# A bidirectional hybrid layer in fp32: one product form for the recurrent projections, one mask product a head, and another order at the start and in the middle norm

## The chip, the cores and the metric

The kernel runs on one core of one Trainium2 chip. The metric is the device time of one execution in microseconds (us). A core has TensorE (PE: matrix products and transpositions, with its weight loads, PEld), VectorE (DVE), ScalarE (ACT), GpSimd (POOL), and SyncE (SP), whose queue issues nearly all DMAs here.

## The reference

One layer on 256 tokens of width 2048, all in fp32:

```python
h = rmsnorm(x, g_pre)
xr, gr, q, k, v, qm, gl = split(h @ w_in)          # 2048 2048 2048 512 512 2048 3*2048
xc = conv4(xr) + b                                  # depthwise, along the tokens
y_lru  = (scan_forward(xc) + scan_backward(xc)) * gelu(gr)      # RG-LRU, gates from xc
y_attn = windowed_gqa(rope(q), rope(k), v)          # 16 heads of 128, |i-j| <= 128, sink logit
y_mem  = cross_attention(qm, rmsnorm(mem) @ w_mem_kv)           # 4 heads of 512
merged = sum(sigmoid(gl_b + b_gate) * (y_b @ w_b) for the three branches)
x = x + rmsnorm(merged @ w_out, g_post)             # "middle norm": this and the next
x = x + rmsnorm(square(relu(rmsnorm(x, g_mlp) @ w_up)) @ w_down, g_mlp_post)
```

## The kernel before, in words

Each fp32 operand of a product is split into a high part (rounded to TensorE's fp32r) and the remainder, and a product is three: high by high, high by low, low by high.

**Weights.** All weight matrices lie in one array of 344 chunks in the order of use, each of two halves of 128x1024 (512 KB). `emit` and `part` load a half on SP's queue (L113), ScalarE rounds it to `wh` (L117), VectorE subtracts to get `wl` (L119). There are six pairs of these tiles, three chunks. `chunk` takes the next one for use, `ahead` issues the one after next, and between the two calls of `emit` it runs `tick`: one step of each of the lists that `later` has put up. By these lists the vector work of the branches (convolution, gates, scans, softmax) is dealt out between the products, in program order on each engine.

**Two forms of a projection of 128 output features.** The activations `hm` of 128 input features are one tile of 512 columns, the high parts of the 256 tokens and then the low parts. `proj` (L157) takes a product of all 512 columns with `wh` for each of the 16 blocks of input features (L151), and one of the 256 high columns with `wl` (L155). Its bank then holds two halves that must be added: `ysum` copies one on ScalarE (L284) and adds the other on VectorE (L285). `proj_one` (L195) takes three products of 256 columns a block (L204 to L206) into half a bank; one VectorE multiplication with the reciprocal norm `rx` evacuates it. The start of the program makes four chunks block by block as the input lands (`quad`).

**Recurrent branch.** `lru_group` runs for four groups of four blocks of features. A group projects four chunks for `xr` and four for the gate `gl`. Group 0 has its `xr` from `quad`, so its form is `proj_one` for the four of `gl`; groups 1 to 3 use it for all eight. `hm` isn't normalized when these products are made, hence `rx` at the end.

**Windowed attention.** For a head and each of two token halves, `head_tasks` makes three products of 256 columns for the scores and adds the far block's mask by a product of a 128-column mask with the identity (L869 to L872).

**Order.** In most of the program a scheduler keeps the order of the code on each engine, with the lists above. In the start and in the middle norm the order of TensorE, ScalarE and VectorE is that of the code exactly.

**Start.** `first_act` loads the input (`xp`, four tiles of four blocks) and the first halves of weights in turn on SP (the first two blocks of `xp` and the two quarters of the first half apart), and TensorE meanwhile does products with ones (`warm`).

**Middle norm.** The last 512 columns of the output projection end in two banks `pst`, one for each half of the tokens (rows 0 and 1). A half's statistic gives `x1` by `x1_part` (L1075), `half_tiles` transposes it (L1086) and splits it, and `half_high` makes the first half products of four chunks of the MLP (L255) for one half of the tokens. The columns from 1024 on are transposed for both halves at once by `feed` (L1103). `quad_lows` and `quad_rest` (L263, L274) are the other products of the four chunks, and then come `proj` calls, the first into the bank that the oldest of the four chunks frees.

Of the kernel before, what the change touches and what calls it, by code (L numbers as in the profile page):

```python
# [15 lines left out]
P = 128  # L16
S = 256
# [46 lines left out]
class Body:  # L64
# [40 lines left out]
    def part(self, src, hi, lo, pieces=1, behind=None, keep=None, hook=None):  # L105
# [3 lines left out]
        for i in range(pieces):  # L109
            if hook is not None and 2 * i == pieces:  # L110
                hook()
# [14 lines left out]
    def emit(self, c, h, pieces=1, behind=None, keep=None, hook=None):  # L126
# [5 lines left out]
        return self.part(self.io["wall"][c, h], wh, wl, pieces, behind, keep, hook)  # L132
# [62 lines left out]
    def proj_one(self, act, spec, pool=None):  # L195
        nc = self.nc
        w = self.chunk(spec)
        ps = self.pmm.tile([P, 2 * S], F32, tag="mm", name="ps") if pool is None else pool.tile(
            [P, 2 * S], F32, tag="sc", name="ps")
        o = ps[:, :S]  # L200
        for k in range(KT):
            wh, wl = (x[:, (k % 8) * P:(k % 8 + 1) * P] for x in w[k // 8])
            a = act[k // 2][:, k % 2, :]
            nc.tensor.matmul(o, wh, a[:, :S], start=(k == 0), stop=False)  # L204
            nc.tensor.matmul(o, wh, a[:, S:], start=False, stop=False)  # L205
            nc.tensor.matmul(o, wl, a[:, :S], start=False, stop=(k == KT - 1))  # L206
        self.ahead()
        return o

    def tok_mms(self, pst, act, ci, w, ts, halves=(0, 1)):  # L210
        nc = self.nc
        for half in halves:
# [75 lines left out]

    def split(self, src, hi, lo):
# [36 lines left out]
    def setup_rest(self):  # L326
# [9 lines left out]
        self.masks = []  # L336
        for t in range(2):
# [7 lines left out]
            mr = c.tile([P, P], F32R, name=f"mask{t}")  # L345
            nc.vector.tensor_copy(mr, m)
            self.masks.append(mr)
# [158 lines left out]
    def first_act(self):  # L506
# [3 lines left out]
        self.warm(8)  # L510
# [10 lines left out]
        def half(i, hook=None):  # L521
            c, h = divmod(i, 2)
            firsts.append(self.emit(c, h, 1 if i else 2, firsts[i - 3] if i > 2 else None, hook=hook))
# [4 lines left out]
        def second():  # L528
            load(1, 1)
            tile_k(1)  # L530

        self.root_ready()
        load(0, 1)
        tile_k(0)
        half(0, second)
# [73 lines left out]
    def lru_group(self, g, hm, ylru, region=None):  # L609
# [26 lines left out]
        if g == 0:  # L636
# [5 lines left out]
            first = self.proj_one(hm, ("F", "w_in", D), self.psc)  # L642
# [4 lines left out]
        else:  # L647
            for b in range(4):
# [208 lines left out]
    def head_tasks(self, head, qa, ka, vh, vl, yattn):  # L857
# [4 lines left out]
        def scores():  # L862
            ps = self.psc.tile([P, 2, S], F32, tag="sc", name="sc")
            kh, kl = self.hl(ka, kv)
            for t in range(2):
                o = ps[:, t, :]
                far = ps[:, t, (1 - t) * P:(2 - t) * P]
                qh, ql = (x[:, t * P:(t + 1) * P] for x in qa)
                nc.tensor.matmul(o, qh, kh, start=True, stop=False)  # L869
# [446 lines left out]
```

## Time and profile before

| | us |
|---|---|
| median of 3 runs (lowest, highest) | 2013.94 (2012.83, 2014.39) |
| the profiled execution | 2013.35 |
| its span in the profile | 2011.6 |
| TensorE busy | 1996.1 (99%) |
| VectorE busy | 1264.4 (63%) |
| ScalarE busy | 1061.4 (53%) |

The span is from the first to the last instruction of the profile. Durations of products overlap, since TensorE is pipelined: its pace is read from starts. A wait is the idle time of an engine before an instruction, put down to what ended it.

### The profile page before, as it was taken

How to read it: one execution, taken by the hardware profiler on the slowest of the kernel's cores; microseconds unless marked ns; L12 is line 12 of the kernel's file. 1: busy time of each engine (PE TensorE's matmuls, PEld its weight loads, DVE VectorE, ACT ScalarE, POOL GpSimd, SP SyncE). 2: the span in 40 equal slices, each digit the busy share in tenths (PEclk: the TensorE clock that was granted, in tenths of full speed). 3: DMA queues.
4: the chain of work that ended last, by engine and by line, in shares of the span. 5: the costliest groups of instructions: out<-in, count | busy, mean ns of one | idle time of the engine just before them, and what ended most of it. 6: DMA issues, size and time to landing. Idle time of an engine off the chain costs nothing.

```text
span 2011.6 us, 27672 instructions
## 1 busy us (share of the span) xinstructions
PE 1996.1 (99%) x10700; PEld 1728.7 (86%) x10700; DVE 1264.4 (63%) x1629; ACT 1061.4 (53%) x1502; POOL 28.1 (1%) x30
## 2 busy tenths in 40 slices
PE   9999999999999999999999999999999999999998
PEld 8999998888888888888888888888888888888886
DVE  7988596876567555655655555575456556555654
ACT  6767667778344444544454444464445445434542
POOL 0000000000022000000000000000000000000000
PEclk9999999999999999999999999999999999999999
DMA  8665565554666655555556566366555555555563
GB/s 276 205 210 177 187 218 178 170 170 154 205 204 220 198 189 183 173 169 180 179 174 199 188 220 210 136 220 198 190 190 189 195 189 188 196 191 189 189 219 105
DMA packets 110405, 383.24 MB, mean 191 GB/s; under 512 B 12864, under 2 KB 15936, under 8 KB 110272
## 3 DMA queue, kind: packets, MB, share of 16 engines
q1 hardware_dynamic: 110128, 381.45, 57.9%
q8 instruction: 84, 1.38, 0.3%
q14 instruction: 49, 0.40, 0.1%
q10 hardware_dynamic: 144, 0.01, 0.0%
HBM read 376.69 MB, written 2.10 MB: 188 GB/s over the span
## 4 chain that ended last, share of the span: by engine, by line
PE 97%; DVE 1%; ACT 0%; DMA 0%; issue 0%; SPq 0%; DVEq 0%; ACTq 0%
PE ps L151 20%; PE pst L220 18%; PE pst L221 18%; PE pst L224 18%; PE ps L155 11%; PE ps L204 3%; PE ps L206 3%; PE ps L205 3%; DVE wl L119 1%; PE tp L830 0%; PE ps L255 0%; DMA xp<-xT 0%; PE gps L673 0%; PE av L843 0%; PE gps L672 0%
## 5 line engine op out<-in xcount | busy, mean ns | idle before, releaser
L119 DVE TENSOR_TENSOR wl<-raw,wh 128x1024 fp32r<-128x1024 f32 (+1 forms) x689 | 846.7, 1232 | 472.8 <-ACT wh L117 466.9
L117 ACT ACTIVATE wh<-raw 128x1024 fp32r<-128x1024 f32 (+1 forms) x689 | 726.2, 1057 | 582.4 <-PE pst L221 504.3
L151 PE MATMUL ps<-h,wh 128*128 128x512 f32 x960 | 229.8, 391 | 0.8 <-DVE y L285 0.8
L151 PEld LDWEIGHTS ps<-h,wh 128*128 128x128 f32 x960 | 176.3, 188 | 35.3 <-DVE y L285 1.2
L220 PE MATMUL pst<-wh,u 128*128 128x512 f32 x512 | 199.2, 389 | 0.0
L221 PE MATMUL pst<-wh,u 128*128 128x512 f32 x512 | 199.2, 389 | 0.0
L284 ACT ACTIVATE evac<-ps 128x256 f32<-128x256 f32 x120 | 45.3, 380 | 247.9 <-PE ps L151 247.9
L220 PE MATMUL pst<-wh,hm 128*128 128x512 f32 x416 | 163.1, 392 | 0.0
L221 PE MATMUL pst<-wh,hm 128*128 128x512 f32 x416 | 162.4, 390 | 0.0
L151 PE MATMUL ps<-hm,wh 128*128 128x512 f32 x576 | 142.8, 392 | 0.0
L224 PE MATMUL pst<-wl,u 128*128 128x512 f32 x512 | 137.5, 389 | 0.0
L204 PE MATMUL ps<-hm,wh 128*128 128x256 f32 x448 | 126.9, 283 | 0.4 <-DVE xr L285 0.4
L155 PEld LDWEIGHTS ps<-h,wl 128*128 128x128 f32 x960 | 123.1, 191 | 4.7
L205 PE MATMUL ps<-hm,wh 128*128 128x256 f32 x448 | 126.8, 283 | 0.0
L206 PE MATMUL ps<-hm,wl 128*128 128x256 f32 x448 | 126.8, 283 | 0.0
L155 PE MATMUL ps<-h,wl 128*128 128x256 f32 x960 | 124.5, 283 | 0.0
L151 PEld LDWEIGHTS ps<-hm,wh 128*128 128x128 f32 x576 | 104.1, 189 | 19.1
L221 PEld LDWEIGHTS pst<-wh,u 128*128 128x128 f32 x512 | 96.1, 188 | 20.0
L224 PEld LDWEIGHTS pst<-wl,u 128*128 128x128 f32 x512 | 96.1, 188 | 20.0
L220 PEld LDWEIGHTS pst<-wh,u 128*128 128x128 f32 x512 | 96.1, 188 | 19.9
L224 PE MATMUL pst<-wl,hm 128*128 128x512 f32 x416 | 111.2, 389 | 0.0
L285 DVE TENSOR_TENSOR y<-ps,evac 128x256 f32<-128x256 f32 x64 | 27.1, 424 | 106.6 <-ACT evac L284 106.6
(261 smaller groups left out, 3108.5 us busy)
## 6 DMA issues: line engine op xcount, KB each, us to landing
raw<-wall SPq DMA_DIRECT2D x687, 512.0 KB, 3.5
raw<-wgate SPq DMA_DIRECT2D x8, 512.0 KB, 4.1
bias<-bgate SPq DMA_DIRECT2D x12, 256.0 KB, 2.9
swap<-ry SPq DMA_DIRECT2D x40, 64.0 KB, 2.5
mp<-memT SPq DMA_DIRECT2D x4, 512.0 KB, 4.9
x<-xt SPq DMA_DIRECT2D x4, 512.0 KB, 4.7
out<-x SPq DMA_DIRECT2D x8, 256.0 KB, 2.1
xp<-xT SPq DMA_DIRECT2D x3, 512.0 KB, 7.2
```

The source lines that it names most:

```text
L117: act = nc.scalar.activation(hi[:, s], raw[:, s], AF.Copy)
L119: nc.vector.tensor_tensor(lo[:, s], raw[:, s], hi[:, s].bitcast(F32), op=ALU.subtract)
L151: self.nc.tensor.matmul(ps, wh, act[k // 2][:, k % 2, :], start=(k == 0), stop=(k == KT - 1))
L155: self.nc.tensor.matmul(ps[:, S:], wl, act[k // 2][:, k % 2, :S], start=False, stop=False)
L204: nc.tensor.matmul(o, wh, a[:, :S], start=(k == 0), stop=False)
L205: nc.tensor.matmul(o, wh, a[:, S:], start=False, stop=False)
L206: nc.tensor.matmul(o, wl, a[:, :S], start=False, stop=(k == KT - 1))
L220: nc.tensor.matmul(pst[t], xh, wh[i], start=(k == 0), stop=False)
L221: nc.tensor.matmul(pst[t], xl, wh[i], start=False, stop=False)
L224: nc.tensor.matmul(pst[t], xs[k, t][0], wl[i], start=False, stop=(k == KT - 1))
L284: self.nc.scalar.activation(t, ps[:, S:2 * S], AF.Copy)
L285: self.nc.vector.tensor_tensor(out, ps[:, :S], t, op=ALU.add)
```

## The change

There are five parts.

1. `proj_one` is gone. The 28 chunks that used it go through `proj`, with `ysum` behind it, and the multiplication by `rx` comes once for four chunks, on a whole page of 128x1024 (`by_rx`). `xr` of groups 1 to 3 is a page now, and its convolutions follow as steps of a list after all four chunks.
2. `proj` can take a bank of the other pool, `psc`. The first two gate chunks of group 0 and the fifth chunk of the MLP use it.
3. In the scores the two mask products of a head become one of 256 columns, over both token halves, between the products of the high and of the low parts of q.
4. In the middle norm the transpositions of the second block of row 0 move between the high and the low products of the last half of the output projection (`between`), those of row 1 move among the products of row 0, and the residuals of the later columns are made whole and earlier.
5. At the start the first half of the weights is one load, ahead of the input, the first two blocks of the input are one load, and `warm(8)` becomes `warm(10)`.

```diff
-    def proj(self, act, spec):
+    def proj(self, act, spec, pool=None):
         w = self.chunk(spec)
-        ps = self.pmm.tile([P, 2 * S], F32, tag="mm", name="ps")
+        ps = self.pmm.tile([P, 2 * S], F32, tag="mm", name="ps") if pool is None else pool.tile(
+            [P, 2 * S], F32, tag="sc", name="ps")
...
+            if between is not None:
+                between()
...
+    def by_rx(self, page):
+        r = self.rx.unsqueeze(1).broadcast_to([P, 4, S])
+        self.nc.vector.tensor_tensor(page, page, r, op=ALU.mult)
...
         self.root_ready()
-        load(0, 1)
+        lows = []
+        half(0, lows)
+        load(0, 2)
         tile_k(0)
-        half(0, second)
+        lows[0]()
+        tile_k(1)
         load(2, 2)
...
-                ps = self.proj_one(hm, ("F", "w_in", (4 * g + b) * P))
-                x = self.t1("xr")
-                nc.vector.tensor_tensor(x, ps, self.rx, op=ALU.mult)
-                self.later([lambda b=b, x=x: conv(b, x)])
+                self.ysum(self.proj(hm, ("F", "w_in", (4 * g + b) * P)), page[:, b, :])
+            self.by_rx(page)
+            self.later(*([lambda b=b: conv(b, page[:, b, :])] for b in range(4)))
...
-            ps = first if g == 0 and b == 0 else self.proj_one(hm, ("F", "w_in", D + (4 * g + b) * P))
-            nc.vector.tensor_tensor(gl[:, b, :], ps, self.rx, op=ALU.mult)
+            spec = ("F", "w_in", D + (4 * g + b) * P)
+            ps = first if g == 0 and b == 0 else self.proj(hm, spec, self.psc if g == 0 and b == 1 else None)
+            self.ysum(ps, gl[:, b, :])
+            if b == 3:
+                self.by_rx(gl)
...
-                nc.tensor.matmul(o, qh, kh, start=True, stop=False)
-                nc.tensor.matmul(far, self.identr, self.masks[t], start=False, stop=False)
-                nc.tensor.matmul(o, qh, kl, start=False, stop=False)
-                nc.tensor.matmul(o, ql, kh, start=False, stop=True)
+                nc.tensor.matmul(ps[:, t, :], q[t][0], kh, start=(t == 0), stop=False, skip_group_check=True)
+                nc.tensor.matmul(ps[:, t, :], q[t][0], kl, start=False, stop=False, skip_group_check=True)
+            far = ps.rearrange("p t s -> p (t s)")[:, P:P + S]
+            nc.tensor.matmul(far, self.identr, self.masks, start=False, stop=False, skip_group_check=True)
+            for t in range(2):
+                nc.tensor.matmul(ps[:, t, :], q[t][1], kh, start=False, stop=True, skip_group_check=True)
...
-            half_tiles(0, 1)
-            self.tok_mms(pst, mg, 3, pair[1], (1,), (1,))
+            self.tok_mms(pst, mg, 3, pair[1], (1,), (1,), lambda: half_tiles(0, 1))
             statistic(1)
...
-            self.half_high(ups, wup, h2, 0, range(8))
+            self.half_high(ups, wup, h2, 0, range(6))
...
             z_gain(1)
+            half_tiles(1, 0)
             z_gain(0)
-            half_tiles(1, 0)
+            self.half_high(ups, wup, h2, 0, range(6, 8))
+            self.half_high(ups, wup, h2, 1, range(1))
             half_tiles(1, 1)
-            self.half_high(ups, wup, h2, 1, range(8))
-            x1_part(1, rows[1], 2, near)
+            self.half_high(ups, wup, h2, 1, range(1, 8))
+            x1_part(1, rows[1], 2, full)
             low(1)
+            x1_part(0, rows[0], 3, full)
             feed(4)
...
-            x1_part(1, rows[1], 2, far)
             feed(5)
+            x1_part(1, rows[1], 3, full)
             low(1)
...
-                    ps = self.proj(h2, ("F", "w_up", q * D + n * P))
+                    ps = self.proj(h2, ("F", "w_up", q * D + n * P), self.psc if q == 0 and n == 4 else None)
```

Three places of the order on the engines. The first is VectorE within the chunks of the second group of the recurrent branch, before: `xr` and `xc` are the projection and its convolution, `T`, `ip` and `a` are pages of the scan's gates.

```order
L119 TENSOR_TENSOR wl<-raw,wh 128x1024
L623 SCALAR_TENSOR_TENSOR xc<-xr,vec,xc 128x254
L651 TENSOR_TENSOR xr<-ps,rstd 128x256
L291 TENSOR_TENSOR xca<-xc,xca 128x256
L119 TENSOR_TENSOR wl<-raw,wh 128x1024
L623 SCALAR_TENSOR_TENSOR xc<-xr,vec,xc 128x255
L119 TENSOR_TENSOR wl<-raw,wh 128x1024
L623 SCALAR_TENSOR_TENSOR xc<-xr,vec,xc 128x255
L623 SCALAR_TENSOR_TENSOR xc<-xr,vec,xc 128x254
L651 TENSOR_TENSOR xr<-ps,rstd 128x256
L712 TENSOR_TENSOR ip<-ip,T 128x1024
L291 TENSOR_TENSOR xca<-xc,xca 128x256
```

The same place after:

```order
L271 TENSOR_TENSOR xr<-ps,evac 128x256
L117 TENSOR_TENSOR wl<-raw,wh 128x1024 x2
L702 TENSOR_TENSOR ip<-ip,T 128x1024
L271 TENSOR_TENSOR xr<-ps,evac 128x256
L117 TENSOR_TENSOR wl<-raw,wh 128x1024
L277 TENSOR_TENSOR xr<-xr,rstd 128x1024
L117 TENSOR_TENSOR wl<-raw,wh 128x1024
L610 SCALAR_TENSOR_TENSOR xc<-xr,vec,xc 128x255 x4
L610 SCALAR_TENSOR_TENSOR xc<-xr,vec,xc 128x254 x2
L117 TENSOR_TENSOR wl<-raw,wh 128x1024
L281 TENSOR_TENSOR xca<-xc,xca 128x256
L271 TENSOR_TENSOR gl<-ps,evac 128x256
```

Each `xr` was multiplied out of its bank and convolved at once; now it is added (L271), the page is multiplied in one (L277), and the convolutions come together behind it.

The second is TensorE in the middle norm, from the last but one half of the output projection on, before. `mg` is the merged input of that projection, `ft` the transposed tiles, `x_11344` and `x_11173` the tiles of the norm's output, `h_...` the pairs of its transposed blocks.

```order
L224 MATMUL pst<-wl,mg 128x512 x2
L1086 MATMUL ft<-ident,x_11344 128x128 x4
L220 MATMUL pst<-wh,mg 128x512
L221 MATMUL pst<-wh,mg 128x512
L220 MATMUL pst<-wh,mg 128x512
L221 MATMUL pst<-wh,mg 128x512
L224 MATMUL pst<-wl,mg 128x512 x2
L255 MATMUL ps<-h_11789,wh 128x2x128 x8
L255 MATMUL ps<-h_11790,wh 128x2x128 x8
L255 MATMUL ps<-h_11791,wh 128x2x128 x8
L255 MATMUL ps<-h_11792,wh 128x2x128 x8
L1086 MATMUL ft<-ident,x_11173 128x128 x4
```

The same after, where the tiles are `x_10931` and `x_10760`:

```order
L210 MATMUL pst<-wl,mg 128x512 x2
L204 MATMUL pst<-wh,mg 128x512
L205 MATMUL pst<-wh,mg 128x512
L204 MATMUL pst<-wh,mg 128x512
L205 MATMUL pst<-wh,mg 128x512
L1076 MATMUL ft<-ident,x_10931 128x128 x4
L210 MATMUL pst<-wl,mg 128x512 x2
L241 MATMUL ps<-h_11376,wh 128x2x128 x8
L241 MATMUL ps<-h_11377,wh 128x2x128 x8
L241 MATMUL ps<-h_11378,wh 128x2x128 x8
L1076 MATMUL ft<-ident,x_10760 128x128 x4
L241 MATMUL ps<-h_11379,wh 128x2x128 x8
```

The first transpositions shown moved down behind four high products, and the two sets that followed the 32 half products (the second of them not shown before) now stand after 24 and after 36 of them.

The third is ScalarE's start, before: `hm` the split input, `wh` the rounded weights.

```order
L278 ACT_TABLE_LOAD
L278 ACTIVATE junk<-eps 128x1
L494 ACTIVATE hm<-xp,vec 128x256
L117 ACTIVATE wh<-raw 128x512
L494 ACTIVATE hm<-xp,vec 128x256
L117 ACTIVATE wh<-raw 128x512
L494 ACTIVATE hm<-xp,vec 128x256 x2
L117 ACTIVATE wh<-raw 128x1024
```

And after:

```order
L264 ACT_TABLE_LOAD
L264 ACTIVATE junk<-eps 128x1
L115 ACTIVATE wh<-raw 128x1024
L482 ACTIVATE hm<-xp,vec 128x256 x4
L115 ACTIVATE wh<-raw 128x1024
L482 ACTIVATE hm<-xp,vec 128x256 x2
```

The first half of the weights is rounded in one piece, before any of the input.

## Rows read from the trace of the kernel before

**Rows 1.** The page: busy time, share of the span and instructions of each engine.
```profile
PE 1996.1 (99%) x10700; PEld 1728.7 (86%) x10700; DVE 1264.4 (63%) x1629; ACT 1061.4 (53%) x1502; POOL 28.1 (1%) x30
```

**Rows 2.** Waits: engine, line, waited for; us in total, times, longest.
```profile
DVE y L285 <- ACT evac L284: 106.6, 58, 1.9
...
PE ft L1103 <- DVE x L1075: 2.2, 2, 1.4
PE ps L183 <- ACT wh L117: 2.2, 3, 1.4
...
PE ps L204 <- DVE xr L285: 0.4, 1, 0.4
DVE ry L285 <- ACT evac L284: 0.4, 1, 0.4
```

**Rows 3.** A window: start:end, us, busy us (instructions) of PE, PEld, DVE, ACT, POOL.
```profile
168.58:214.66 46.08, 46.08 (x386) 46.07 (x385) 44.31 (x65) 29.48 (x36) 0.00 (x0) 1.00 0.69 213
```

**Rows 4.** The chain in order of time: start us, us, what.
```profile
1478.52 3.65 PE ps L151 x16
...
1484.09 3.65 PE ps L151 x16
```

**Rows 5.** Instructions on tile xr: ns min/median/max, first and last start, forms.
```profile
L651 DVE TENSOR_TENSOR xr<-ps,rstd x12: 411/417/425, 91.2 to 276.6; 128x256 f32<-128x256 f32 x12
L285 DVE TENSOR_TENSOR xr<-ps,evac x4: 417/418/420, 38.1 to 39.1; 128x256 f32<-128x256 f32 x4
```

**Rows 6.** Timeline, VectorE and TensorE: start us, us, engine, line, operation.
```profile
113.32 1.22 DVE L119 TENSOR_TENSOR wl<-raw,wh 128x1024 fp32r<-128x1024 f32 x1
...
121.42 0.28 PE L206 MATMUL ps<-hm,wl 128*128 128x256 f32 x1
```

**Rows 7.** Timeline of TensorE at one head of the windowed attention.
```profile
449.27 0.60 PE L830 MATMUL tp<-ident,pr 128*128 128x128 f32 x4
449.62 0.36 PE L869 MATMUL sc<-kact,qa 128*128 128x256 f32 x1
...
450.64 0.40 PE L220 MATMUL pst<-wh,hm 128*128 128x512 f32 x1
```

**Rows 8.** Timeline of TensorE in the middle norm, and one row of VectorE.
```profile
1288.44 0.63 PE L224 MATMUL pst<-wl,mg 128*128 128x512 f32 x2
...
1289.76 0.48 PE L220 MATMUL pst<-wh,mg 128*128 128x512 f32 x1
...
1291.24 3.99 PE L255 MATMUL ps<-h,wh 128*128 128x256 f32 x32
...
1292.93 1.42 DVE L1075 SCALAR_TENSOR_TENSOR x<-z,tot,x 128x512 f32<-128x512 f32 x2
...
1295.06 1.09 PE L1086 MATMUL ft<-ident,x 128*128 128x128 f32 x8
1296.39 4.09 PE L255 MATMUL ps<-h,wh 128*128 128x256 f32 x32 [0.25 <-DVE h L495]
...
1318.78 1.09 PE L274 MATMUL ps<-h,wh 128*128 128x512 f32 x4
1320.66 1.66 PE L151 MATMUL ps<-h,wh 128*128 128x512 f32 x6 [0.78 <-DVE y L285]
```

**Rows 9.** Timeline of TensorE at the start.
```profile
0.99 3.79 PE L481 MATMUL warm<-ones 128*128 128x128 f32 x16 [0.99 <-POOL eps L309]
5.06 1.41 PE L183 MATMUL ps<-hm,wh 128*128 128x512 f32 x4 [0.28 <-ACT wh L117]
...
7.44 1.20 PE L183 MATMUL ps<-hm,wh 128*128 128x512 f32 x4 [0.49 <-ACT wh L117]
...
13.86 1.19 PE L183 MATMUL ps<-hm,wh 128*128 128x512 f32 x4
```

**Rows 10.** The chain at the start.
```profile
1.65 0.42 SPq L514
...
4.01 7.91 DMA xp<-xT
```

More of the change, by code (lines that the diff above doesn't have):

```diff
@@ L103, in drain, with part @@
             self.tick()
-    def part(self, src, hi, lo, pieces=1, behind=None, keep=None, hook=None):
+    def part(self, src, hi, lo, pieces=1, behind=None, keep=None):
         nc = self.nc
@@ L109, in part @@
         for i in range(pieces):
-            if hook is not None and 2 * i == pieces:
-                hook()
             s = slice(i * n, (i + 1) * n)
@@ L124, in part, with emit @@
         return act
-    def emit(self, c, h, pieces=1, behind=None, keep=None, hook=None):
+    def emit(self, c, h, pieces=1, behind=None, keep=None):
         if c >= NCH or (c, h) in self.held:
@@ L131, in emit @@
         self.held[c, h] = (wh, wl)
-        return self.part(self.io["wall"][c, h], wh, wl, pieces, behind, keep, hook)
+        return self.part(self.io["wall"][c, h], wh, wl, pieces, behind, keep)
     def ahead(self):
@@ L193, in quad, with tok_mms @@
         return ps
[L195 to L210, printed above, removed]
+    def tok_mms(self, pst, act, ci, w, ts, halves=(0, 1), between=None):
         nc = self.nc
@@ L335, in setup_rest @@
         nc.vector.tensor_copy(self.identr, self.ident)
-        self.masks = []
+        self.masks = c.tile([P, S], F32R, name="masks")
         for t in range(2):
@@ L344, in setup_rest @@
             )
-            mr = c.tile([P, P], F32R, name=f"mask{t}")
-            nc.vector.tensor_copy(mr, m)
-            self.masks.append(mr)
+            nc.vector.tensor_copy(self.masks[:, t * P:(t + 1) * P], m)
     def rates(self):
@@ L509, in first_act @@
         pages = [self.page_fp("xp") for _ in range(4)]
-        self.warm(8)
+        self.warm(10)
         nc.scalar.dma_start(self.vec[:, :KT], self.io["vec"][:, :KT])
@@ L519, in tile_k, with half @@
             self.scaled_split(pages[k // 4][:, k % 4, :], self.v("norm_mix_pre", k), *self.hl(hm, k))
-        def half(i, hook=None):
+        def half(i, keep=None):
             c, h = divmod(i, 2)
-            firsts.append(self.emit(c, h, 1 if i else 2, firsts[i - 3] if i > 2 else None, hook=hook))
+            firsts.append(self.emit(c, h, 1, firsts[i - 3] if i > 2 else None, keep=keep))
         def square(p):
             nc.scalar.activation(pages[p], pages[p], AF.Square)
-        def second():
-            load(1, 1)
-            tile_k(1)
         self.root_ready()
-        load(0, 1)
+        lows = []
+        half(0, lows)
+        load(0, 2)
         tile_k(0)
-        half(0, second)
+        lows[0]()
+        tile_k(1)
         load(2, 2)
@@ L641, in lru_group @@
                 self.ysum(pss[b], xs[b])
-            first = self.proj_one(hm, ("F", "w_in", D), self.psc)
+            first = self.proj(hm, ("F", "w_in", D), self.psc)
             self.token_scale()
@@ L647, in lru_group @@
         else:
+            page = self.page_fp("xr")
             for b in range(4):
-                ps = self.proj_one(hm, ("F", "w_in", (4 * g + b) * P))
-                x = self.t1("xr")
-                nc.vector.tensor_tensor(x, ps, self.rx, op=ALU.mult)
-                self.later([lambda b=b, x=x: conv(b, x)])
+                self.ysum(self.proj(hm, ("F", "w_in", (4 * g + b) * P)), page[:, b, :])
+            self.by_rx(page)
+            self.later(*([lambda b=b: conv(b, page[:, b, :])] for b in range(4)))
         for b in range(4):
-            ps = first if g == 0 and b == 0 else self.proj_one(hm, ("F", "w_in", D + (4 * g + b) * P))
-            nc.vector.tensor_tensor(gl[:, b, :], ps, self.rx, op=ALU.mult)
+            spec = ("F", "w_in", D + (4 * g + b) * P)
[3 more added lines that the diff above has]
+                self.by_rx(gl)
             if b % 2 == 0:
@@ L864, in scores @@
             kh, kl = self.hl(ka, kv)
+            q = [[x[:, t * P:(t + 1) * P] for x in qa] for t in range(2)]
             for t in range(2):
-                o = ps[:, t, :]
-                far = ps[:, t, (1 - t) * P:(2 - t) * P]
-                qh, ql = (x[:, t * P:(t + 1) * P] for x in qa)
-                nc.tensor.matmul(o, qh, kh, start=True, stop=False)
-                nc.tensor.matmul(far, self.identr, self.masks[t], start=False, stop=False)
-                nc.tensor.matmul(o, qh, kl, start=False, stop=False)
-                nc.tensor.matmul(o, ql, kh, start=False, stop=True)
+                nc.tensor.matmul(ps[:, t, :], q[t][0], kh, start=(t == 0), stop=False, skip_group_check=True)
[4 more added lines that the diff above has]
+                nc.tensor.matmul(ps[:, t, :], q[t][1], kh, start=False, stop=True, skip_group_check=True)
             box["ps"] = ps
@@ L1163, in run @@
             self.quad_lows(ups, wup, h2, range(4))
-            x1_part(1, rows[1], 2, far)
             feed(5)
+            x1_part(1, rows[1], 3, full)
             low(1)
             self.quad_lows(ups, wup, h2, range(4, 8))
-            x1_part(0, rows[0], 3, full)
             wup.append(self.chunk(ups_specs[2]))
             low(1)
-            x1_part(1, rows[1], 3, full)
             self.quad_rest(ups, h2, wup, range(8, 9))
```

## The prediction

> **What bounds the kernel now.** I read the busy shares first: TensorE 99% of the span, VectorE 63%, ScalarE 53% [rows 1]. So the change can pay only where TensorE works for less time or stands less; what happens on the other engines counts only if TensorE comes to wait for it. The waits come next [rows 2]: those of TensorE are short and lie at the start (2.2 us for weights in three waits, 0.4 us for `xr`) and in the middle norm (2.2 us for `x`). The largest of VectorE, 106.6 us in 58 waits for the copy of a product, holds up nobody, but it matters for a rival. Then I read the pace of the products in a window and in the chain, and last the gaps of TensorE in the middle norm and at the start.
>
> **Part 1, the 512-column form (28 chunks).** Before, eight such chunks are the window from 168.58 to 214.66, in which TensorE is never idle [rows 3]: 46.08 / 8 = 5.760 us a chunk, and 5.760 / 48 = 0.120 us a product of 256 columns. The other form, 16 products of 512 columns and 16 of 256, takes from 1478.52 to 1484.09 in the chain, where nothing waits: 5.567 us (3.65 / 16 = 0.228 and 1.91 / 16 = 0.119 a product) [rows 4]. TensorE saves 0.193 us a chunk, 28 x 0.193 = 5.4 us, all on the path that sets the end.
> The Trainium skill ("TensorE: Matmul & The Clock Gate", section "Back-to-back issue gap") gives N/2.4 + 2.5 ns as the gap of single products, with the remark that a stream can differ. An estimate from that page is 215.8 ns for 512 columns and 109.2 for 256, a saving of 0.04 us a chunk and 1.2 us in all. The rows have 228 and 120 ns, some 13 ns over the columns for each product and not 2.5, so the trace decides for the larger saving.
> The price is on VectorE. Each chunk had one multiply (417 ns) and now has one add (417 ns) [rows 5] that must wait for ScalarE's copy, and a group of four is then multiplied by the norm as one page of 128x1024. For this the nearest row is the subtraction of `wl`, of the same shape, at 1.22 us [rows 6]; I take that (it lies between 1.2 and four multiplies of 0.42, 1.7). A stretch of eight has two of them. VectorE is busy 44.31 of 46.08 us there [rows 3], so it wants 44.31 + 2.44 = 46.75 us in 46.08 - 1.55 = 44.53: 2.2 us too much. What hides it is the lead of the weights: a `wl` made from 113.32 to 114.54 is first used at 121.42, 6.9 us later [rows 6]. I take 0; without this cover it costs 3 x 2.2 = 6.6 us. It can't gain: VectorE does no less than before. ScalarE's eight copies more don't bind, it is busy 29.48 of 46.08 [rows 3].
> The second gate chunk of the first group gets a bank of the other pool, so TensorE need not wait for the bank that `xr` frees: 0.4 us [rows 2], and with it the restart, which at the end of the middle norm is 0.2 (0.97 us lost there for 0.78 waited, part 3). I take 0.6, between 0.3 and 0.8.
>
> **Part 2, the scores (16 heads).** A head's eight products take 449.62 to 450.64, 1.02 us [rows 7]. Six products of 256 columns and one mask product of 256, at 0.12 each, make 0.84; the first one behind transpositions may start 0.08 late as it does now. So 0.10 to 0.18 a head; I take 0.106, 16 x 0.106 = 1.7 us, between 0.8 (half of it lost at the changes of weights) and 2.9. Nothing else moves: the maximum over the scores reads the same bank as before.
>
> **Part 3, the middle norm.** Four transpositions among products take 0.35 us, as 449.27 to 449.62 shows for the same size [rows 7]. TensorE loses time in five places [rows 8]. 1288.44 to 1289.76 holds two low products (0.46) and four transpositions (0.35): 0.51 lost. 1295.06 to 1296.39 holds eight transpositions (0.70): 0.63 lost. The two waits for `x` at later transpositions are 2.2 us [rows 2] and, with a restart of 0.2 each, 2.6. 1318.78 to 1320.66 holds four products (0.91): 0.97 lost. In all 4.7 us, the most that can go.
> I follow the new order. The transpositions of half 0,1 stand behind the high products of the last half, when their `x` is there: the first place closes, and TensorE is done with the output projection at 1290.63 in place of 1291.24 [rows 8]. But the splits of these four blocks come some 0.2 us later, ScalarE takes the second statistic behind them, and the first residual of row 1, which now starts at 1292.93 and takes 0.71, is ready at about 1293.9. TensorE has done six of eight parts of the first half at 1290.63 + 6/8 x 3.82 = 1293.5 (3.82 = 1295.06 - 1291.24): 0.4 us of wait, and I add 0.25 (the wait at 1296.39) at the one part of the second half and again at the next transpositions, since both need splits just made. These 0.9 us eat what the first two places gave (1.1); the second half ends 0.1 to 0.2 earlier. Behind it the residuals of columns 1024 to 2047 are whole and come earlier, so the two waits for `x` go (2.6), and the fifth projection has a bank of its own, so the last wait goes (0.97). What is late next: the subtraction for the ninth chunk now stands behind a residual; I take 0.4 us of wait. Sum 0.15 + 2.6 + 0.97 - 0.4 = 3.3; I take 3.2. Bounds: -0.8 if the early waits are twice as long and the later ones stay, 4.7 if no new wait comes.
>
> **Part 4, the start.** The first half chunk is now one load ahead of `xp`, and the first two blocks of `xp` come as one. Before, TensorE starts products at 5.06 and 7.44 [rows 9], stands 2.2 us in three waits [rows 2], and begins its fifth group at 13.86. What must have landed for the first product now is what had to for the second group, so it moves from 5.06 to about 7.4 to 7.7, and the groups run on without the idle 2.2 us. The work of the first four groups is 13.86 - 5.06 - 2.2 = 6.6; from 7.7 it ends at 14.3, which is 0.5 later than before. The other end is all idle gone, 2.2 earlier. Two issues fewer stand ahead of the block that the chain waits for, at 0.42 us each; but the chain waits 7.91 us for its bytes [rows 10], which are as many as before, so I take half of that gain, 0.4 us (-0.5 to 2.2). The four more warm products end at about 5.7, before any data of the new order is there, and cost nothing.
>
> **Sum.** 5.4 + 0.6 + 1.7 + 3.2 + 0.4 = 11.3 us. The profiled execution took 2013.35 (span 2011.6 and 1.75 around it), so 2002.0. The median of the runs lies 0.6 above it, which I leave to the range.
>
> **The rivals.**
> All better: no new wait in the middle norm (4.7) and 2 us at the start: 2002.0 - 1.5 - 1.6 = 1998.9. For it: each wait that I added rests on a single row. Chance 0.08.
> The middle norm saves nothing, because the statistic of row 1 and not TensorE sets the time there: 2005.2. For it: VectorE and ScalarE have as much to do between the same two ends. Against it: the two longest waits [rows 2] are for late residuals that the new order moves ahead of subtractions not yet wanted. Chance 0.11.
> The start goes wrong: the products begin at the lower level of the clock (1.2 GHz), as TensorE now stands some 2 us between the warm products and the first group. Against it: an idle stretch of up to 1.4 us [rows 2] passed there, and the groups on both sides of it, at 7.44 and 13.86, took the same 1.2 us [rows 9]. The Trainium skill ("TensorE: Matmul & The Clock Gate", section "Why this matters for your kernels") says that idle gaps between bursts bring the lower clock back; no run here shows it. Half of the 6.6 us of work at half the clock costs 3.3 us and the 0.4 goes: 2005.7; with the change of level somewhat earlier, 2004.5. Chance 0.05.
> The 512-column form saves nothing, because columns alone set the pace and both forms have 12,288 of them in a chunk: 2002.0 + 5.4 = 2007.4. By the formula of the Trainium skill that part 1 quotes it would be 2006.2. Against it stand the two rates measured [rows 3, 4]. Chance 0.03.
> Slower: VectorE, which works in order, now waits for ScalarE's copy in each of the eight chunks. Where such adds wait, the mean is 106.6 / 58 = 1.84 us [rows 2]; eight make 14.7, with the overflow 16.9, less the lead of 6.9 it is 10 us a stretch, 30 in three: 2032. It decides once waits and overflow pass the 6.9 us of lead. For it: VectorE has 1.8 us to spare in 46. Against it: the 20 adds of `ry`, which stand among the same kind of work, waited 0.4 us in all [rows 2], since a busy VectorE comes to an add after the copy is done. Chance 0.06, half of it within 0.2% of before, where a third of that price is paid.
>
> **How the numbers follow.** Forecast 0.67, with a range of its own of 2000.0 to 2004.5. To hold the better case (0.08), the middle norm (0.11) and the start (0.05) as well, the range is 1999.0 to 2006.5; some 0.15 lies outside it. 0.2% (4 us) is about what a measurement can tell from no change. Faster by more than that: 0.67 + 0.08 + 0.11 + 0.05 + 0.03 = 0.94; within it 0.03; slower 0.03.
>
> **What would show it.** Eight chunks of the recurrent projections take 44.5 us with no wait of TensorE for `wl` or `xr`; a head's scores take 0.84 to 0.92; the wait for `x` at the later transpositions is gone, shorter waits (0.25 to 0.5) stand around the first two half products of the MLP, and from the end of the output projection to the fifth projection of the MLP it is some 2.6 us less; the first product comes at 7.3 to 7.7 and the fifth group at 13.4 to 13.9. A wait for `wl` or a copy in the stretches of eight would make the prediction wrong.

## The result and the profile after

The changed kernel takes 2002.26 us (median of 6 runs, 2001.10 to 2002.71), the kernel before 2013.65 (6 runs, 2012.83 to 2014.39): a ratio of 0.9943, 95% interval 0.993 to 0.9955, or 11.4 us less. The profiled execution after took 2002.71 us, with a span of 2000.9 (2011.6 before).

The page and the waits of the kernel after answer to [rows 1, 2]. The engines' busy shares hardly move, TensorE is busy for 7.3 us less:

```profile
PE 1988.8 (99%) x10240; PEld 1705.7 (85%) x10240; DVE 1270.2 (63%) x1634; ACT 1068.7 (53%) x1529; POOL 28.1 (1%) x30
```

Waits (engine, line, waited for: us in total, times, longest us):

```profile
DVE y L271 <- ACT evac L270: 107.0, 58, 1.9
...
PE ps L182 <- DVE hm L483: 1.6, 1, 1.6
...
PE ps L260 <- DVE wl L117: 0.2, 1, 0.2
```

The waits for `x` and for `xr` are gone from TensorE, the three at the start have become one of 1.6 us, and one of 0.2 us for a `wl` is new.

Where the time went is read best from the starts of the same work of TensorE in the two timelines:

| work of TensorE | before | after | earlier by | gained since the line above |
|---|---|---|---|---|
| first projection behind the four chunks of the start | 31.40 | 31.19 | 0.21 | 0.21 |
| sums for `rx`, behind that projection | 37.14 | 36.77 | 0.37 | 0.16 |
| second gate chunk | 38.56 | 37.44 | 1.12 | 0.75 |
| end of the last stretch of eight chunks | 299.49 | 293.28 | 6.21 | 5.09 |
| first scores | 354.95 | 348.71 | 6.24 | 0.03 |
| behind the windowed attention | 493.83 | 486.10 | 7.73 | 1.49 |
| first transposition of the middle norm | 1287.08 | 1279.35 | 7.73 | 0.00 |
| first down projection of the MLP | 1387.59 | 1376.27 | 11.32 | 3.59 |
| last down projection | 1915.91 | 1904.59 | 11.32 | 0.00 |

So TensorE gains 11.3 us in five places and nothing in between. From the last down projection to the end of the span it is 95.7 us before and 96.3 after, so the two profiled executions differ by a little less, 10.7. The change doesn't touch this last part: it takes 95.6 to 96.35 us in the fourteen traces of this document, without regard to the edit.

A stretch of eight chunks, to be held against [rows 3] (start:end, us, busy us of PE, PEld, DVE, ACT, POOL with instructions, then the granted clock):

```profile
165.48:210.01 44.53, 44.53 (x257) 39.37 (x256) 42.55 (x64) 30.92 (x43) 0.00 (x0) 1.00 0.66 206
```

It takes 44.53 us for 46.08, with 256 weight loads in the window in place of 385. VectorE is busy 42.55, not more than before.

A head, to be held against [rows 7]: the scores take 442.26 to 443.17, 0.91 us for 1.02.

```profile
441.91 0.60 PE L820 MATMUL tp<-ident,pr 128*128 128x128 f32 x4
442.26 0.36 PE L857 MATMUL sc<-kact,qa 128*128 128x256 f32 x1
...
443.17 0.40 PE L204 MATMUL pst<-wh,hm 128*128 128x512 f32 x1
```

The middle norm on TensorE, to be held against [rows 8]:

```profile
1282.99 3.04 PE L241 MATMUL ps<-h,wh 128*128 128x256 f32 x24
1286.16 0.65 PE L1076 MATMUL ft<-ident,x 128*128 128x128 f32 x4
1286.57 1.87 PE L241 MATMUL ps<-h,wh 128*128 128x256 f32 x12
1288.29 0.76 PE L1076 MATMUL ft<-ident,x 128*128 128x128 f32 x4
1288.80 3.59 PE L241 MATMUL ps<-h,wh 128*128 128x256 f32 x28
1292.23 0.60 PE L1093 MATMUL ft<-ident,x 128*128 128x128 f32 x4
...
1296.93 1.09 PE L260 MATMUL ps<-h,wh 128*128 128x512 f32 x4
1298.24 0.74 PE L260 MATMUL ps<-h,wl 128*128 128x256 f32 x4 [0.21 <-DVE wl L117]
...
1308.54 1.09 PE L260 MATMUL ps<-h,wh 128*128 128x512 f32 x4
1309.46 1.98 PE L149 MATMUL ps<-h,wh 128*128 128x512 f32 x8
```

The start, to be held against [rows 9], and the windows of it (the granted clock is the third figure from the end):

```profile
0.99 4.25 PE L469 MATMUL warm<-ones 128*128 128x128 f32 x20 [0.99 <-POOL eps L299]
6.88 1.20 PE L182 MATMUL ps<-hm,wh 128*128 128x512 f32 x4 [1.64 <-DVE hm L483]
8.02 1.17 PE L187 MATMUL ps<-hm,wl 128*128 128x256 f32 x4
8.98 1.91 PE L182 MATMUL ps<-hm,wh 128*128 128x512 f32 x4
...
14.35 1.09 PE L182 MATMUL ps<-hm,wh 128*128 128x512 f32 x4
```

```profile
7.00:8.00 1.00, 1.00 (x4) 0.55 (x4) 1.00 (x2) 0.65 (x2) 0.00 (x0) 1.00 1.04 414
8.00:9.00 1.00, 1.00 (x6) 0.98 (x6) 1.00 (x3) 0.65 (x2) 0.00 (x0) 0.55 1.01 414
9.00:11.00 2.00, 2.00 (x7) 1.61 (x7) 1.51 (x3) 0.67 (x1) 0.00 (x0) 0.50 1.04 412
11.00:12.00 1.00, 1.00 (x6) 0.92 (x6) 0.29 (x1) 0.83 (x3) 0.00 (x0) 0.74 1.00 401
12.00:14.00 2.00, 2.00 (x13) 1.73 (x12) 1.54 (x3) 2.00 (x5) 0.00 (x0) 1.00 0.92 348
```

The first group runs at the full clock. (The trace's first record of the granted clock stands at 4.69 us; ahead of a first record the column shows 1.00 whatever the pace. The warm products start 213 ns apart up to there and 111 behind it.) From some point past 8 us to past 11 us the granted clock is 0.50, the lower of the two levels, and four products of 512 columns take 1.7 us (8.98 to 10.69) in place of 0.93.

### The profile page after: what moved, and what is told of

Read it like the earlier page. It is cut to its first block, busy times and chain, and to the rows that moved or that the text cites. A ratio compares the mean times of both kernels' runs of the same rounds, so it can differ in the third digit from the quotient of the medians.

```text
span 2000.9 us, 26757 instructions
## 1 busy us (share of the span) xinstructions
PE 1988.8 (99%) x10240; PEld 1705.7 (85%) x10240; DVE 1270.2 (63%) x1634; ACT 1068.7 (53%) x1529; POOL 28.1 (1%) x30
## 4 chain that ended last, share of the span: by engine, by line
PE 99%; DVE 0%; DMA 0%; ACT 0%; issue 0%; DVEq 0%; SPq 0%; ACTq 0%
PE ps L149 26%; PE pst L205 18%; PE pst L204 18%; PE pst L210 18%; PE ps L153 13%; PE ps L182 1%; PE ps L260 1%; PE tp L820 0%; PE ps L187 0%; PE gps L663 0%; PE av L833 0%; PE gps L662 0%; PE av L832 0%; PE gps L661 0%; PE av L831 0%; PE ps L241 0%
## 5 line engine op out<-in xcount | busy, mean ns | idle before, releaser
L117 DVE TENSOR_TENSOR wl<-raw,wh 128x1024 fp32r<-128x1024 f32 x688 | 846.3, 1234 | 453.9 <-ACT wh L115 447.7
L115 ACT ACTIVATE wh<-raw 128x1024 fp32r<-128x1024 f32 x688 | 725.2, 1058 | 556.2 <-PE pst L205 500.4
L149 PE MATMUL ps<-hm,wh 128*128 128x512 f32 x1024 | 250.9, 392 | 0.0
L149 PEld LDWEIGHTS ps<-hm,wh 128*128 128x128 f32 x1024 | 186.4, 189 | 35.0
L270 ACT ACTIVATE evac<-ps 128x256 f32<-128x256 f32 x148 | 55.9, 380 | 268.6 <-PE ps L149 268.6
L153 PEld LDWEIGHTS ps<-hm,wl 128*128 128x128 f32 x1024 | 131.3, 191 | 5.1
L153 PE MATMUL ps<-hm,wl 128*128 128x256 f32 x1024 | 132.8, 283 | 0.0
L271 DVE TENSOR_TENSOR y<-ps,evac 128x256 f32<-128x256 f32 x64 | 27.2, 424 | 107.1 <-ACT evac L270 107.0
L210 PEld LDWEIGHTS pst<-wl,hm 128*128 128x128 f32 x416 | 78.1, 188 | 16.3
```

Of the source, the lines that this page charges most:

```text
L115: act = nc.scalar.activation(hi[:, s], raw[:, s], AF.Copy)
L117: nc.vector.tensor_tensor(lo[:, s], raw[:, s], hi[:, s].bitcast(F32), op=ALU.subtract)
L149: self.nc.tensor.matmul(ps, wh, act[k // 2][:, k % 2, :], start=(k == 0), stop=(k == KT - 1))
L153: self.nc.tensor.matmul(ps[:, S:], wl, act[k // 2][:, k % 2, :S], start=False, stop=False)
L210: nc.tensor.matmul(pst[t], xs[k, t][0], wl[i], start=False, stop=(k == KT - 1))
L270: self.nc.scalar.activation(t, ps[:, S:2 * S], AF.Copy)
```

## The experiments

Each is the changed kernel with one edit, unless it says more. Starts are compared with those of the changed kernel behind the start, since the start itself varies from one execution to the next, as the first four show.

**Warm products until the input is there.**

```diff
-        self.warm(10)
+        self.warm(18)
```

> The changed kernel with 18 pairs of warm products in place of 10, so that TensorE works until about 6.8 us and goes over to the first product at 6.88 without standing. In the changed kernel it stands 1.64 us there, and the granted clock is 0.50 to 0.55 from about 8.3 to 11.3 us. Theory (the idle time brings the lower clock; the landing of the last quarter of the input takes back a part): clock 1.00 throughout, the fifth group begins at 13.0 to 13.4 in place of 14.35, but the thirteenth must wait for its weights split at 24.9, so the first chunk behind the four begins 0.3 to 0.7 us earlier than 31.19; time 2001.6 to 2001.9. Rival 1 (nothing behind binds): 1.0 to 1.6 us earlier. Rival 2 (the clock falls whatever TensorE did before): clock 0.5 again, 0 us.

2001.98 us (5 runs, 2001.46 to 2002.42), ratio to before 0.9941 (0.9927 to 0.9954). TensorE begins the groups 0.8 us later and is through 1.0 us earlier:

```profile
7.65 1.17 PE L182 MATMUL ps<-hm,wh 128*128 128x512 f32 x4
8.66 0.63 PE L187 MATMUL ps<-hm,wl 128*128 128x256 f32 x4
...
30.17 1.98 PE L149 MATMUL ps<-hm,wh 128*128 128x512 f32 x8
```

The granted clock is 1.00 in every window, and its first record, at 6.52 us, is ahead of the first group. The first chunk behind the four comes at 30.17 for 31.19, so nothing behind took the gain back, as I had thought the last quarter of the input would: it lands when it lands, and ScalarE's split of it began at 22.25 us in the changed kernel and at 21.43 here, with the same loads. Rival 1 has the size of this trace right. The runs can't tell the two kernels apart.

**Fewer warm products** (`warm(8)`).

> The changed kernel with 8 pairs of warm products, as before the change: TensorE stands from 4.5 to 6.88 us, 2.4 us in place of 1.9. Theory (idle time brings the lower clock): the stretch at 0.5 is there again, at least as long, and the first chunk behind the four begins 0 to 0.6 us later than 31.19. Rival (the drop has nothing to do with the warm products): same times to 0.1 us.

One run of 2002.64. The clock is 0.50 from 8 to 11 us again and the first chunk comes at 31.10, as with ten pairs. The times are the rival's. But later traces with ten pairs have the first chunk anywhere from 29.94 to 31.19, so one trace of each doesn't show that two pairs more or less are without effect.

**The start of before.**

```diff
-        half(0, lows)
-        load(0, 2)
+        load(0, 1)
         tile_k(0)
-        lows[0]()
-        tile_k(1)
+        half(0, second)
```

> The changed kernel with the start of before: input first, the first half of the weights in two loads, 8 pairs of warm products. All else as changed. Theory (the part is worth what the traces show at the first chunk behind the four, 31.40 before and 31.19 after): 0.2 us later than the changed kernel, clock 1.00 throughout, groups at 5.1, 7.4, 10.5, 12.3 and 13.9. Rival (the start is worth the 0.4 us forecast, the rest being lost elsewhere): 0.4 us.

One run of 2001.49. The column of the clock shows 1.00 and the first chunk comes at 30.70: not 0.2 us later than the changed kernel but 0.5 earlier. (The clock's first record stands at 6.59 us, and the first four products take 1.75, at half pace; those of the kernel before take 1.25, with the record at 5.56.) Its third group stands at 9.67, in the kernel before at 10.50, with the same code. So a single pair of traces can't weigh the start. The later experiments have the changed start too, and their first chunks come at 29.94, 30.01, 31.00, 30.93, 30.72 and 30.85 where the column shows 1.00, and at 31.18 where the clock fell. The old start has 31.40 and 30.70. Of a gain of the new start nothing is shown.

**Two moves in the middle norm, with 18 pairs of warm products.**

```diff
+            x1_part(1, rows[1], 3, full)
             feed(5)
-            x1_part(1, rows[1], 3, full)
...
-            self.emit(nxt + 2, 0, keep=lows)
             z_gain(1)
             half_tiles(1, 0)
+            self.emit(nxt + 2, 0, keep=lows)
```

> The changed kernel with 18 pairs of warm products and two moves in the middle norm: the last residual of row 1 stands ahead of the transposed blocks of the second feed on VectorE and not behind them, and the weights of the third chunk of the MLP are rounded on ScalarE behind the splits of row 1 and not ahead of them. Theory: 0.3 to 0.7 us from the start, 0.3 to 0.4 from the wait before the low products of the ninth block (1296.93 to 1298.24 now for 0.92 of products), 0.2 to 0.4 from the waits at the transpositions of row 1 (0.31 and 0.29 now): in all 0.8 to 1.5 us less than the changed kernel, 2000.8 to 2001.5. Rival (the rounding that moved back is late for its products): the middle norm is no shorter and the wait only moves to the low products, 2001.6 to 2002.

2001.63 us (5 runs, 2001.33 to 2002.47), ratio 0.9939 (0.9927 to 0.9952). In its trace the start gives 0.9 and the ninth block 0.3, as the residual no longer waits behind the feed; the waits at the transpositions of row 1 stay as they were, so the rounding on ScalarE was not what held them. The runs can't tell this kernel from the changed one either.

**The form of 256 columns back** in all 28 chunks (`proj_one` and the multiplication by `rx` for each), banks as changed.

> The changed kernel with the 28 chunks back in the form of 48 products of 256 columns and one multiplication by rx each; both banks of the other pool, the start, the scores and the middle norm stay as changed. Theory (0.19 us a chunk, VectorE hidden in both forms): a stretch of eight takes 46.1 us for 44.5, the end of the last stretch of eight comes 5.2 to 5.4 us later than the changed kernel, time 2007.4 to 2007.8. Rival 1 (columns alone set the pace, the gain of these stretches comes from the order of VectorE): under 1 us. Rival 2 (the second gate chunk's bank is part of what the stretch gives): 6 us.

2006.50 us (5 runs, 2006.07 to 2007.44), ratio 0.9964 (0.995 to 0.9978). From the sums behind the first chunk to the end of the last stretch TensorE loses 5.2 us against the changed kernel, 0.19 us in each of 27 chunks. A stretch of eight is back at 46.08, with TensorE never idle:

```profile
166.46:212.54 46.08, 46.08 (x385) 46.07 (x384) 44.31 (x65) 29.52 (x36) 0.00 (x0) 1.00 0.67 214
```

The total is 1 us under the 2007.4 expected; in the profiled execution the granted clock stayed at 1.00 and the start was 1.1 us earlier than in the changed kernel's; one trace doesn't tell why the median is lower, and 1 us lies within the interval. Both rivals fall: the loss is 5.2, neither under 1 nor 6, and though the edit brings VectorE's old order back as well, TensorE waits for VectorE in the stretch in neither form.

**All projections in the first pool.**

```diff
-self.proj(hm, spec, self.psc if g == 0 and b == 1 else None)
+self.proj(hm, spec)
...
-self.proj(h2, ("F", "w_up", q * D + n * P), self.psc if q == 0 and n == 4 else None)
+self.proj(h2, ("F", "w_up", q * D + n * P))
```

> The changed kernel with all projections in banks of the first pool again: the second gate chunk of the first group and the fifth chunk of the MLP wait for the bank that the first evacuated block frees. Theory: 0.7 to 0.8 us later at the second gate chunk (0.75 between the traces of before and after at that place) and 0.9 to 1.0 us later at the fifth chunk of the MLP, in all 1.6 to 1.8 us. Rival (with the new form or the new order the bank is free in time): under 0.5 us.

One run of 2003.23. The two waits are back, the rows of TensorE's list:

```profile
PE ps L149 <- DVE y L271: 0.8, 1, 0.8
PE ps L149 <- DVE xr L271: 0.6, 1, 0.6
```

The starts lose 0.91 us at the second gate chunk and 1.08 at the fifth chunk of the MLP; at the first down projection TensorE is 1.9 us later, a little over the 1.6 to 1.8 expected. The same trace has the changed start with the clock at 1.00 after a longer wait than the changed kernel's own:

```profile
6.86 1.19 PE L182 MATMUL ps<-hm,wh 128*128 128x512 f32 x4 [1.66 <-DVE hm L483]
```

```profile
8.00:9.00 1.00, 1.00 (x7) 0.96 (x7) 1.00 (x3) 0.94 (x1) 0.00 (x0) 1.00 1.03 422
9.00:11.00 2.00, 2.00 (x12) 1.69 (x11) 1.42 (x4) 0.57 (x2) 0.00 (x0) 1.00 1.03 420
```

**The two mask products of before.**

```diff
+                nc.tensor.matmul(far, self.identr, self.masks[:, t * P:(t + 1) * P], start=False, stop=False)
...
-            nc.tensor.matmul(far, self.identr, self.masks, start=False, stop=False, skip_group_check=True)
```

> The changed kernel with two mask products of 128 columns a head as before. Theory: 0.10 us a head, first head to the last 1.5 to 1.7 us later than the changed kernel. Rival (what the heads gave is the order of the products and not their number, or the vector work behind the scores): under 0.8 us.

One run of 2003.32. Each head loses 0.07 to 0.10 us, from the first head's scores to the end of the attention 1.49. The edit brings back both the number of the mask products and their place, so this run doesn't tell the two apart; that the order alone would give it isn't excluded.

**The middle norm of before**, with the fifth chunk still in the other pool.

> The changed kernel with the order of the middle norm as before, but the fifth chunk of the MLP still in the other pool. Theory (the later residuals give 2.6 us, the first two places next to nothing, as new waits eat them, less 0.4 at the ninth block): 2.4 to 2.8 us later than the changed kernel, of which 0.1 to 0.4 come before the end of the second half product block. Rival (the first transpositions between products are what pays): over 1.0 us before the end of that block.

One run of 2004.75. It loses 2.5 us behind the start, 0.4 of it before the end of the second half product block, and the wait for `x` is back as it was in [rows 2]:

```profile
PE ft L1093 <- DVE x L1065: 2.2, 2, 1.4
```

**Transpositions ahead of the last half, not inside it.**

```diff
-            self.tok_mms(pst, mg, 3, pair[1], (1,), (1,), lambda: half_tiles(0, 1))
+            half_tiles(0, 1)
+            self.tok_mms(pst, mg, 3, pair[1], (1,), (1,))
```

> The changed kernel with the transpositions of the second block of row 0 again ahead of the last half of the output projection and not between its high and its low products; all else in the middle norm as changed. Theory (the statistic of row 1 through ScalarE and VectorE sets when the next transpositions can start, so that what TensorE saves ahead of it is waited for behind): 0 to 0.3 us later at the end of the second half product block. Rival (what is saved there stays saved): 0.5 to 0.7 us later.

One run of 2001.98. The place itself costs 0.5 us again: 0.56 from the transpositions to the next product, and the half products begin at 1282.98, as late as in the changed kernel (1282.99) though the start was 0.5 us ahead of it.

```profile
1280.95 0.81 PE L1076 MATMUL ft<-ident,x 128*128 128x128 f32 x4
1281.51 0.47 PE L204 MATMUL pst<-wh,mg 128*128 128x512 f32 x1
...
1282.98 3.03 PE L241 MATMUL ps<-h,wh 128*128 128x256 f32 x24
1285.84 0.60 PE L1076 MATMUL ft<-ident,x 128*128 128x128 f32 x4
1286.20 1.73 PE L241 MATMUL ps<-h,wh 128*128 128x256 f32 x12
1287.76 0.75 PE L1076 MATMUL ft<-ident,x 128*128 128x128 f32 x4
```

But they then take 2.86 to the next transpositions (3.17 in the changed kernel) and 1.56 to those after (1.72): at 1287.76 the lead is the 0.5 us of the start again. Nothing is lost.

**More work on VectorE.**

```diff
         self.nc.vector.tensor_tensor(page, page, r, op=ALU.mult)
+        for _ in range(2):
+            self.nc.vector.tensor_tensor(page, page, page, op=ALU.max)
```

> The changed kernel with two more VectorE instructions of 128x1024 on each of the seven pages behind the multiplication by rx (a maximum of the page with itself, results unchanged): four more in a stretch of eight, 4.9 us. Theory (the lead of wl, 8 us at its least in the changed kernel, covers what VectorE has too much): no wait of TensorE for wl, stretches of 44.5 us, no difference. Rival (VectorE has no cover left once it is busy throughout): 2 to 4 us a stretch.

One run of 2002.14. There is no new wait of TensorE and no difference behind the start: the cover holds for 4.9 us more in a stretch. The lead of the weights pays for it: at its least in the stretches it falls from 7.9 us to 4.8 (a `wl` done at 285.28 is first used at 290.12). With `range(8)`:

> The same with eight more of them on each page: sixteen in a stretch of eight, 19.5 us. Theory: VectorE was busy 42.0 to 42.6 of 44.5 us, so 17 us too much meet 8 us of lead: 5 to 9 us a stretch, 15 to 27 us in all, with waits of TensorE for wl. Rival (work that nobody waits for is put off further and the lead is longer than 8 us as a whole): under 5 us in all.

One run of 2022.0. TensorE loses 19.5 us: 5.2, 4.6 and 7.5 up to the ends of the three stretches and 2.2 behind the last. The size lies in the theory's range, the place isn't the theory's:

```profile
PE pst L204 <- DVE gl L271: 12.5, 3, 5.8
PE pst L210 <- DVE wl L117: 2.4, 1, 2.4
```

12.5 of the 15 us are for a bank that the add of a group's first gate chunk empties late, since VectorE comes to it behind the instructions on the page of `xr`, and only 2.4 for a `wl`. Most of the other 4.6 us is TensorE's clock, which the theory didn't have: behind the two longest waits, of 4.37 and 5.80 us, it is at its lower level, and products of 512 columns start 0.43 us apart and not 0.23. Half the pace for the 3.1 and 4.5 us of work in these two windows costs 3.8 us by my estimate:

```profile
310.59 0.77 PE L204 MATMUL pst<-wh,hm 128*128 128x512 f32 x1 [5.80 <-DVE gl L271]
311.16 0.63 PE L205 MATMUL pst<-wh,hm 128*128 128x512 f32 x1
311.58 0.63 PE L204 MATMUL pst<-wh,hm 128*128 128x512 f32 x1
```

```profile
219.51:222.93 3.42, 3.12 (x7) 2.49 (x8) 3.42 (x9) 1.28 (x2) 0.00 (x0) 0.50 0.05 19
308.26:315.09 6.83, 4.50 (x11) 3.57 (x12) 6.56 (x16) 3.59 (x7) 0.00 (x0) 0.50 0.40 121
```

The two shorter waits of the same trace, 2.42 and 2.34 us, left the clock at 1.00.

**The best of it together**: 14 pairs of warm products, the moves of the fourth experiment, and the transpositions of row 1 ahead of both products with the gain on VectorE (`half_tiles(1, 0)` ahead of `z_gain(1)`).

> The kernel with the two moves in the middle norm, with 14 pairs of warm products in place of 18, and with the transpositions and splits of row 1 ahead of both products of the last output columns with the gain on VectorE. Theory (the clock holds over an idle time of some 0.5 us; the first product at 6.9 us and not 7.7; the split of row 1 no longer behind a 0.7 us product): first chunk behind the four at 29.4 to 30.1 in place of 30.2 to 30.3, 0.2 to 0.4 us less in the middle norm; 2000.5 to 2001.4. Rival 1 (the clock falls again): a stretch at 0.5 and 31.0. Rival 2 (the weights' split for the last quarter of the input binds): no earlier than 30.2.

2001.76 us (5 runs, 2000.83 to 2001.86), ratio 0.9941 (0.9927 to 0.9954). The clock is 1.00 throughout and the first chunk comes at 29.65, 1.5 us before the changed kernel's:

```profile
0.99 4.98 PE L469 MATMUL warm<-ones 128*128 128x128 f32 x28 [0.99 <-POOL eps L299]
6.78 1.19 PE L182 MATMUL ps<-hm,wh 128*128 128x512 f32 x4 [0.81 <-DVE hm L483]
...
29.65 1.98 PE L149 MATMUL ps<-hm,wh 128*128 128x512 f32 x8
```

In the middle norm the last move loses 0.1 us at the transpositions of row 1, and the ninth block keeps its 0.3.

TensorE reaches the last down projection 1.7 us earlier than in the changed kernel. In the runs that is 0.5 us, with intervals that overlap: it beats the kernel before, and against the changed one it is not shown.

## Why the prediction was right

The forecast was 11.3 us and the runs have 11.4. That the sum fits better than its terms is luck, as their errors of 0.15 to 0.4 us cancel. By its steps:

**Part 1** held: 5.4 forecast, 5.25 between the traces (0.16 + 5.09) and 5.2 by the experiment that puts the old form back. That VectorE would want 46.75 us in a stretch was too much; the window has 42.55, since some of its work slides past the end of the stretch: two instructions of 1.2 us on pages of the gates (`gl<-gl,ip` and `ip<-ip`) stand in the window before and not in the one after, and only one of the two multiplications by `rx` lies in it. TensorE waits for none of it. The rival on the slower side had VectorE wait for ScalarE's copies in the eight chunks; in the trace after, no add of `xr` or `gl` waits for one, and the 107.0 us are the adds of `y`, as before. VectorE as the new bound exists and needs far more: 4.9 us on top of a stretch cost nothing, 19.5 cost 5 to 8. What decides then is not the lead of `wl`, as the rival had it, but the bank that the add of a group's first gate chunk empties. The bank of the second gate chunk was put too low: 0.6 forecast, 0.75 between the traces and 0.91 by taking it back.

**Part 2** was mis-sized by a little: 1.7 forecast, 1.49 between the traces and by taking it back, 0.09 a head. The scores themselves give what was forecast, 1.73 (15.96 us in 16 heads before, 14.23 after). About 0.2 of it is lost between them, where the step had nothing else move.

**Part 3** held in its mechanism, 3.2 forecast and 3.59 measured. The early waits were forecast at 0.4 + 0.25 + 0.25. In the timeline of after, counting 0.12 a product and 0.35 for four transpositions, they are 0.3 before 1286.16, 0.45 around 1288.29 and 0.15 elsewhere up to 1292.23, together 0.9; and taking the transpositions out of the products costs nothing, so the first place was worth nothing, as the steps had it. (The steps' 1290.63 is 0.1 too early by their own sum, 0.51 from 1291.24; the traces have 0.52, 4.16 us to 3.64 from the first transposition to the half products.) Up to the end of the second half product block the gain is 0.37, where the steps had 0.15. The later residuals and the moves among row 0's products are 2.5, the bank of the fifth chunk 1.1. The wait before the low products of the ninth block is 0.39 (1296.93 to 1298.24 for 0.92), forecast 0.4.

**Part 4** came out near its size (0.4 forecast, 0.21 between the traces) by luck: over several executions no gain is shown. The step said that the groups run on; the first product came at 6.88, earlier than the 7.4 to 7.7 forecast, but the fifth group at 14.35 and not at 13.4 to 13.9. The work of the first four groups, 6.6 us in the step, is 5.9 where the clock held (6.86 to 12.78 in the kernel with one pool) and 7.5 in the changed kernel. The rival with a chance of 0.05, the lower clock, took place in the profiled execution, though later than the rival had it: the first group ran at full pace, and the 0.50 came behind it and a wait of 1.64 us. It cost about 1 us (the first chunk at 31.19, and at 30.01 in the kernel with one pool, which had waited as long), and not the 2.5 to 3.7 of its price. The traces with warm products until the input don't have it. In the two executions whose products did begin at the lower level the first chunk comes at 30.93 and 30.85, so the price was too high there as well. The step also took one execution's landing times as fixed; the old start varies by 0.7 us at the first chunk, the new one by 1.25.
The Trainium skill ("TensorE: Matmul & The Clock Gate", section "Why this matters for your kernels") has idle gaps bring the lower clock back, gaps longer than any at the start here. The trace of the larger load on VectorE agrees: the clock is 0.50 where TensorE goes on after 4.37 and 5.80 us. At the start the clock fell behind shorter ones too, 1.64, 2.11 and 1.84 us (the changed kernel, eight pairs of warm products, and the larger load), and it stayed at 1.00 behind 1.66 us in the kernel with one pool and behind 2.34 and 2.42 us later under the larger load.

## What to carry to other kernels

Where the profile shows TensorE at its pace for 99% of the span, count its products and read the time from start to start in a stretch without waits: 16 x 0.228 + 16 x 0.119 against 48 x 0.120 gave the largest term to within 3%. Follow a closed gap on to the next point where that engine meets another: the transpositions moved inside products saved 0.5 us that were waited for 3 us later. A part whose effect lies within the spread of the input's landing can't be weighed by one pair of traces; put the old part back into the new kernel and look at several executions.

## What the runs showed of the hardware

The same start code gave three courses in eight profiled executions (the changed kernel and the seven with its start unchanged). In four TensorE is at full pace from the first group. In two it is at half pace from the first group until about 10 us, with 1.87 and 1.88 us for the first four products. In two it is at full pace, then at a granted clock of 0.50 until past 11 us (the kernel with eight warm pairs did the same).

The trace's first record of the clock tells the second course from the others. It stands at 10.15 and 10.18 us there and at 4.47 to 6.21 us in the other six; up to it the column shows 1.00 while the products go at half pace, in the warm products 213 ns apart where the faster ones go 111. So the two executions at half pace had not lost the full clock but not yet got it, after the same 20 warm products as the others.

Where TensorE worked until the input was there, or stood 0.8 us, all three executions kept the full pace. Behind 4.37 and 5.80 us the clock fell. What chooses between the courses at waits of 1.0 to 2.4 us was not settled.
